# Scaling the second half's residual rows in products four and five of the down projections, and alternating rotary and gate items

## The chip, the core and the metric

The kernel runs on one core of a Trainium2 chip. The metric is device time in microseconds (us) of one execution, the median over runs. The engines by the names that the profile uses: PE multiplies matrices, DVE does elementwise work with one or two tensors as input, ACT elementwise functions of one tensor, POOL is a third elementwise engine, and SP issues most of the DMAs (POOL and ACT have DMA queues too). All work between PE's matmuls and the DMAs goes through SBUF, and PE's sums lie in PSUM.

## What is computed

Two layers over a sequence of 1024 rows of width 1024, in float32. Layer 0 mixes with a gated DeltaNet, layer 1 with retention; each is followed by a feed-forward block with a causal convolution of width 3 on its gate. The part of the reference that matters here:

```python
for i in range(DEPTH):
    mod = (e @ ada_w[i] + ada_b[i])[:, None, :]
    sh1, sc1, g1, sh2, sc2, g2 = jnp.split(mod, 6, axis=-1)
    y = mixers[i % N_MIXERS](x * (1.0 + sc1) + sh1)
    x = layer_norm(DN_ALPHA * x + (1.0 + g1) * y, ln_g[i, 0], ln_b[i, 0])
    y = conv_ffn(x * (1.0 + sc2) + sh2, ffn_up[i], ffn_conv_w[i], ffn_conv_b[i], ffn_down[i])
    x = layer_norm(DN_ALPHA * x + (1.0 + g2) * y, ln_g[i, 1], ln_b[i, 1])
```

`conv_ffn` is an up projection to 2 x 2816 columns, the convolution, `silu(gate) * up`, and a down projection from 2816 to 1024. Retention projects to queries, keys, values and a gate, turns queries and keys by rotary tables (`t1 * cos - t2 * sin`, `t1 * sin + t2 * cos`), and multiplies its output by `silu(gate)`.

## The kernel before, in words

A float32 matrix product is made of three matmuls. Each operand is split into a high and a low part: ACT copies it (L89) into a shorter float format, and DVE subtracts that copy from it (L90). Both read and write SBUF. The three products of high and low parts are summed in PSUM.

The large projections use the scheme of Strassen and Winograd: seven products of half-size blocks in place of eight, with sums of blocks as operands. `strassen` walks over a list of items, one for each pair of column blocks; `wino` makes the seven products of an item and hands the results in quadrants to the item's `sink`, which does what follows the projection. Of one item the weights are loaded and summed on DVE (L1213), split (L89, L90) and multiplied (84 matmuls, L110 to L112 and L1163), and the quadrants are put together on DVE (L1154).

**The feed-forward block.** The last sink of an up pair (`gated`, L1570ff) makes four blocks of `silu(gate) * up`, stores those three that the down projection needs as they are, and then makes four sums of them, on POOL for all pairs but the first (L1585), each stored too. The down projection is `proj_gen` (L1276ff): seven products, here numbered one to seven (`p` is 0 to 6 in the code), each of 11 steps (`nj`), each step of 12 matmuls (L285 to L287 or L1437). For a step `ops` loads a block `ar` of the stored activations (L1270), and takes a block of weights (loaded by L1303, summed on DVE at L1311 to L1317); both are split, `ar` into `ab` and the weights into `bb`. The steps' operands are prepared ahead of PE, as far as the number of buffers allows.

For the layer norm that follows, `xload` (L280) loads the residual rows: those of the first half are called up in product three, those of the second in product six. The residual is itself the output of a layer norm whose gain and bias are still to be applied. For rows of the first half `finish` applies them. For rows of the second half `gain_half(n)` (L1339 to L1346) does it in the background in eight pieces of 128 x 512: SP loads a piece (L1343), POOL multiplies by the row of gains and adds the row of biases (L1345 twice), and POOL's own DMA queue stores it (L1346), from where `xload(1, t)` reads it. The pieces are called up inside the loop over steps, in products one and two at every second step, and stand in `lane` buffers. The gain and bias rows occupy four `auh` buffers until the last piece is done. `gain_half` runs in both down projections, about 1198 to 1418 us and 2729 to 2948 us of the span. The second is the end of the program.

**The order of the work.** Engines execute in order; so does SP, so that a DMA that waits for a buffer holds up those behind it. The code is traced in the order written, with generators that interleave streams, and a scheduler then places the instructions by the data and buffers that they wait for. A tile is a numbered buffer of a named group (`lane`, `xT`, `auh`, `qkv`, ...); a new tile of a group waits until the oldest is free. The group `xT` (four tiles of 128 x 512) serves the opening of the kernel.

**Retention's projections of queries, keys and gate.** Layer 1 begins with a `strassen` list of 16 items, about 1450 to 1776 us: gates 0 and 2, then eight rotary items (`rope_item`, L1637ff: for each of two halves DVE does six operations with the rotary tables, L1651 to L1656, and ACT's queue stores the result, L1658), then gates 4 to 14 (`gate_item`, L1663ff: ACT applies Silu, L1667, and stores, L1668). The rotary tables `trig` (L1632) lie in `auh` buffers. `bg_step` calls up, between items, pieces of another background job: `unit` and `gain` (L387 to L395) scale the residual of the next layer norm on POOL as `gain_half` does, and need `auh` buffers for their two rows. The value products of retention (`ret_v`, L651) follow the list.

The lines that the steps of the prediction touch are L1343, L1345, L1346 (pieces), L1585 (sums), L89 and L90 (splits), L280 (residual rows), L1651 to L1656 (rotary tail), L387 and L393 to L395 (background scaling). In the program after the change all lines behind L1669 are three higher.

Of the kernel before, what the change touches and what calls it, by code (L numbers as in the profile page):

```python
# [15 lines left out]
P = 128  # L16
# [3 lines left out]
HALF = 512  # L20
NCH = S // P
GH = 8
RH = 4
# [10 lines left out]
def trunk_kernel(ctx: ExitStack, tc, A):  # L34
# [11 lines left out]
    def tl(tag, shape, dt=F32, name=None):  # L46
        return sb.tile(shape, dt, tag=tag, name=name or tag, bufs=BUFS[tag])
# [13 lines left out]
    def mm_tile():  # L61
        return ps.tile([P, HALF], F32, tag="mm", name="mm", bufs=2)

    def sc_tile():
        return ps.tile([P, HALF], F32, tag="sc", name="sc", bufs=2)

    def acc4():
        return [acc_tile(), acc_tile(), acc_tile(), acc_tile()]
# [13 lines left out]
    def hs(half):  # L82
        return slice(half * HALF, (half + 1) * HALF)
# [4 lines left out]
    def split(dst_h, dst_l, src, eng=dve):  # L88
        act.activation(dst_h, src, AF.Copy)  # L89
        eng.tensor_tensor(dst_l, src, dst_h, ALU.subtract)  # L90
# [3 lines left out]
    def after(key):  # L94
        return tc.issue_after(anchor[key].ins) if key in anchor else nullcontext()
# [12 lines left out]
    def mm3(acc, w, k, hl, first, last, mm=pe.matmul):  # L108
        wh, wl = w
        mm(acc, wl[:, k], hl[0], start=first, stop=False)  # L110
        mm(acc, wh[:, k], hl[1], start=False, stop=False)  # L111
        mm(acc, wh[:, k], hl[0], start=False, stop=last)  # L112
# [262 lines left out]
    xg = [dr.tile([S, D], F32, tag=f"xg{i}", name=f"xg{i}") for i in range(3)]  # L375
# [30 lines left out]

    def build_T(B, xts, scale, shift, tags):
        tags = dict(zip(("T1", "T2", "T3", "T4", "22"), tags))
        tags["12"] = tags["T1"]
        for nm in tags:  # L410
            B[nm] = [None] * 4

        def put(nm, k, src, eng=dve):
            t = two(tags[nm], F32R, nm)
            split(t[0], t[1], src, eng)
            B[nm][k] = t

# [18 lines left out]
        def whole(b, k):  # L436
            pt = mm_tile()
            for i, x in enumerate(B[b][k]):
                pe.matmul(pt, one, x, start=(i == 0), stop=(i == 1))
# [99 lines left out]
    xT = {}  # L539
# [166 lines left out]
    def take(tag, n):  # L706
        while free[tag] < n:
            yield lambda: free[tag] >= n
        free[tag] -= n

    def give(tag, n):
        free[tag] += n
# [444 lines left out]
    def strassen(hT0, xts, scale, shift, items, tags=("hTb", "hTb", "qkv", "qkv", "aux"), direct=False):  # L1157
        B = {"11": hT0[:4], "21": hT0[4:]}
        nblk = [0]
# [7 lines left out]
        def side(n, s):  # L1167
            out = []
            for u in items[n][:2]:
# [4 lines left out]
                for i, b in enumerate((("11", "21"), ("12", "22"))[s]):  # L1174
                    for k in range(4):
                        mm3(X, w, k + 4 * i, B[b][k], i == 0 and k == 0, i == 1 and k == 3)
                out.append(X)
# [96 lines left out]
    def proj_gen(nj, ablk, wsrc, slots, xsrc, G, final, ln_next, tag, ltags, dst, key, mm=pe.matmul, gate=None, gain=None):  # L1274
# [60 lines left out]
        xts = [[], []]  # L1335
# [2 lines left out]

        def gain_half(n):  # L1339
            hf, rs = n // 4, slice(HALF + n % 4 * P, HALF + (n % 4 + 1) * P)  # L1340
            x = tl("lane", [P, HALF], name="xg")
            with after("w"):
                sp.dma_start(x, gain[1][rs, hs(hf)])  # L1343
            for r, op in zip(grows, (ALU.mult, ALU.add)):
                pool.tensor_tensor(x, x, r[hf], op)  # L1345
            pool.dma_start(xsrc[rs, hs(hf)], x)  # L1346
# [10 lines left out]
        def finish(half, t, nh, c):  # L1357
            dve.tensor_tensor(c, c, G[nh], ALU.mult)
            xv = xts[half][t][:, hs(nh)]
            dve.scalar_tensor_tensor(xv, xv, ALPHA, c, ALU.mult, ALU.add)  # L1360
            dve.bn_stats(stats[half][t][:, nh], xv)
# [85 lines left out]
        for p, (an, bn, fin, side, fresh) in enumerate(prods):  # L1447
            if gate and p < 2 or banks[side] is None:
                banks[side] = acc4() if gate and p < 2 or side == 0 else [sc_tile(), sc_tile(), mm_tile(), mm_tile()]
                if gate and p == 1:  # L1450
                    banks[0] = banks[1]
                    banks[1] = None
            accs = banks[0] if gate and p == 1 else banks[side]
            tail = []
            depth = ltags[3] if p == 6 else 2
            for j in range(nj):
                if gate and p < 2:
                    yield gate(j)
                    yield from take("qkv", 2)
                    give("qkv", 2)  # L1460
                a, w = ops(an, bn, j, not gate and p < (7 if final else 5))
                with after("a"):
                    for st in steps[p * nj + j + ahead:p * nj + j + ahead + 1]:
                        load_b(*st)
                if gain and p < 2 and j % 2 == 0 and p * 4 + j // 2 < 8 and j < 8:
                    gain_half(p * 4 + j // 2)
                if gain and p == 2 and j % 2 == 0 and j < 8:
                    xload(0, j // 2)
                if p == 2 and j < 4 and gate:
                    xload(0, j)  # L1470
                    finish(0, j, 0, c11[j])
                if j >= nj - depth:
                    tail.append((j, a, w))
                else:
                    for t in range(4):
                        mma(accs[t], t, a, w, fresh and j == 0, False, mm if p < 2 else pe.matmul if fresh else mm_on)
                        yield 0.0
                for _ in range(-(-20 // (nj - 1)) if p == 6 else 4 if p == 5 else 2):
                    if later:
                        later.pop(0)()  # L1480
                if p == 5 and j > 1 and not later:
                    for _ in range(-(-16 // (nj - 2))):
                        if hooks:
                            hooks.pop(0)()
                bg_step()
            while later:
                later.pop(0)()
            if p == 5:
                while hooks:
                    hooks.pop(0)()  # L1490
            if p == 6:
                pin[0] = None
            for t in range(4):
                for j, a, w in tail:
                    mma(accs[t], t, a, w, fresh and j == 0, j == nj - 1, mm if p < 2 else pm_on if p == 6 else pe.matmul if fresh else mm_on)
                fin(t, accs[t])
                yield 0.0
            if p == 1:
                yield "P2"
            if p == 4:  # L1500
                hooks = [] if final else ln_hooks(0, xts[0], tag, ln_next, outs, dst, key, bal["h"])
                hooks += [lambda t=t: xload(1, t) for t in range(4)]
# [113 lines left out]
    h0, xts = layer_tail(0, raws, A["gdn_wout"], xin, xs[0], xs[1], next0, False)  # L1616
# [22 lines left out]
    def rope_item(h, j):  # L1639
        def start():  # L1640
            c = {}

            def sink(q, a, b):
                c[q] = c_of(q, a, b)
                hf = q % 2
                if hf not in c or hf + 2 not in c:
                    return
                x1, x2 = c[hf], c[hf + 2]
                cos, sin = trig(h, j)
                m = tl("lane", [P, 2, HALF], name="rm")  # L1650
                dve.tensor_mul(m[:, 0], x2, sin[hf])  # L1651
                dve.tensor_mul(m[:, 1], x1, sin[hf])
                dve.tensor_mul(x1, x1, cos[hf])
                dve.tensor_mul(x2, x2, cos[hf])
                dve.tensor_sub(x1, x1, m[:, 0])
                dve.tensor_add(x2, x2, m[:, 1])  # L1656
                for d, x in enumerate((x1, x2)):
                    act.dma_start(qd[j, h, d][:, hs(hf)], x)  # L1658
            return sink
        u = 8 * j + 2 * h  # L1660
        return A["ret_wqk"][u], A["ret_wqk"][u + 1], start, None

    def gate_item(u):
        def start():
            def sink(q, a, b):
                c = c_of(q, a, b) if b is not None else tl("cv", [P, 516], name="sg")[:, 0:HALF]
                act.activation(c, a if b is None else c, AF.Silu)  # L1667
                act.dma_start(gd[u + q // 2][:, hs(q % 2)], c)  # L1668
            return sink  # L1669
        return A["ret_wg"][u], A["ret_wg"][u + 1], start, None  # L1670

    sc_r, sh_r = next0()
    B = strassen(h0, xts, sc_r, sh_r, [gate_item(0), gate_item(2)]
                 + [rope_item(h, j) for h in range(RH) for j in range(2)] + [gate_item(u) for u in range(4, 16, 2)], ("hTa", "aux", "qkv", "qkv", "hTa"), True)
    hT = [h0, []]
    xlo = []
    for t in range(4):
        x = tl("cv", [P, 516], name="xlo")[:, 0:HALF]
# [270 lines left out]
```

## Time and profile before

| what | value |
|---|---|
| median of three runs | 2973.52 us (2968.97 to 2977.79) |
| span of the profiled execution | 2967.8 us |
| time of the profiled execution itself | not recorded beside its span |
| mean granted PE clock | 0.985 |
| ACT busy | 1316.5 us (44%) |
| moved by DMA | 451.01 MB, mean 152 GB/s |

The span runs from the first to the last instruction of one execution, so it is shorter than a timed run, which also holds what lies around it. The profile's page gives each engine's busy time, the span in 40 slices, the DMA queues, the chain of waits that ended last, and groups of equal instructions. The trace can be asked further: windows (busy time of each engine in a stretch, with the granted clock of PE as a share of full speed and the share of time in which the 16 DMA engines were busy), timelines (start, duration, engine, line, operation, output<-inputs, shape, and in brackets the idle time before it with what ended it), and groups by tile (count; least, median and largest duration in ns; first and last start).

### The profile page before, as it was taken

What the parts mean: (1) busy time and instruction counts of PE and PEld (TensorE: products, weight loads), DVE (VectorE), ACT (ScalarE), POOL (GpSimd) and SP (SyncE); (2) the same over time, 40 slices, a digit from 0 to 9 for tenths busy, and PEclk for the clock granted to TensorE, in tenths of its full rate; (3) what the DMA queues carried; (4) which work ended last, traced back from release to release, by engine and by line L of the source; (5) the groups of instructions that cost most, each with busy time, mean ns of one, the idle gap of its engine ahead of it and who ended that gap; (6) DMA issues with size and microseconds to landing.
All of it is one profiled execution on the core that took longest, in us unless ns stands there. A gap on an engine that the chain in (4) does not pass through costs nothing. (4 is left out here: it accounts for less than half of the span.)

```text
span 2967.8 us, 38939 instructions
## 1 busy us (share of the span) xinstructions
PE 2820.5 (95%) x13638; PEld 2304.5 (78%) x13638; DVE 2242.4 (76%) x4005; ACT 1316.5 (44%) x2413; POOL 474.8 (16%) x469
## 2 busy tenths in 40 slices
PE   8999898999999999999999999999999999999997
PEld 7887777887788888787877887777777788887786
DVE  5787787656688888879678645666689887777979
ACT  4744564444544444446433442222344544444443
POOL 0312221100001111610000202322202011112301
PEclk9999999999999999999999999999999999999998
DMA  7231222254245445865333544665664243335753
GB/s 275 79 113 65 86 79 79 83 167 160 91 158 163 158 151 174 305 198 179 120 128 117 181 160 152 203 189 175 205 212 157 91 135 107 107 107 176 274 183 137
DMA packets 244404, 451.01 MB, mean 152 GB/s; under 512 B 23088, under 2 KB 76592, under 8 KB 244208
## 3 DMA queue, kind: packets, MB, share of 16 engines
q1 hardware_dynamic: 213088, 401.07, 41.0%
q10 hardware_dynamic: 29760, 43.00, 4.0%
q0 software_dynamic: 1360, 4.46, 0.4%
q8 instruction: 107, 1.75, 0.3%
q14 instruction: 89, 0.73, 0.1%
HBM read 339.91 MB, written 108.53 MB: 151 GB/s over the span
## 5 line engine op out<-in xcount | busy, mean ns | idle before, releaser
L651 PE MATMUL acc<-hT,wh 128*128 128x512 f32 x960 | 299.3, 393 | 0.0
L1437 PE MATMUL acc<-bb,ab 128*128 128x512 f32 x984 | 231.4, 393 | 6.6 <-DVE bb L90 5.4
L1585 POOL TENSOR_TENSOR o<-o 128x512 f32<-128x512 f32 x80 | 110.7, 1394 | 716.4 <-DVE o L1578 490.8
L1437 PEld LDWEIGHTS acc<-bb,ab 128*128 128x128 f32 x984 | 182.6, 188 | 50.2 <-DVE bb L90 10.2
L1163 PE MATMUL acc<-T,wb 128*128 128x512 f32 x840 | 203.1, 391 | 6.7 <-DVE wb L90 6.7
L651 PEld LDWEIGHTS acc<-hT,wh 128*128 128x128 f32 x960 | 181.9, 190 | 34.1
L651 PE MATMUL acc<-hT,wl 128*128 128x512 f32 x480 | 201.1, 419 | 0.0
L89 ACT ACTIVATE ab<-ar 128x512 fp32r<-128x512 f32 x210 | 129.6, 625 | 152.7 <-PE mm L287 36.9
L90 DVE TENSOR_TENSOR ab<-ar,ab 128x512 fp32r<-128x512 f32 x210 | 161.9, 777 | 41.1 <-ACT ab L89 41.1
L1163 PEld LDWEIGHTS acc<-T,wb 128*128 128x128 f32 x840 | 157.0, 188 | 43.2 <-DVE wb L90 9.8
L90 DVE TENSOR_TENSOR wl<-wr,wh 128x1024 fp32r<-128x1024 f32 x95 | 119.7, 1260 | 69.6 <-ACT wh L89 68.6
L90 DVE TENSOR_TENSOR wb<-mm,wb 128x512 fp32r<-128x512 f32 x216 | 145.5, 682 | 31.2 <-ACT wb L89 30.6
L90 DVE TENSOR_TENSOR wb<-wr,wb 128x512 fp32r<-128x512 f32 x162 | 111.1, 691 | 69.8 <-ACT wb L89 69.1
L89 ACT ACTIVATE wh<-wr 128x1024 fp32r<-128x1024 f32 x95 | 100.7, 1061 | 132.3 <-PE acc L651 53.1
L1224 ACT ACTIVATE pc<-acc 128x512 f32<-128x512 f32 x143 | 84.9, 593 | 160.7 <-PE acc L1163 97.4
L1564 DVE SCALAR_TENSOR_TENSOR o<-g,vc,o 128x512 f32<-128x512 f32 (+2 forms) x176 | 145.4, 843 | 4.7 <-ACT o L1559 4.1
L89 ACT ACTIVATE wb<-mm 128x512 fp32r<-128x512 f32 x216 | 124.0, 595 | 51.9 <-DVE mm L1213 50.3
L89 ACT ACTIVATE wb<-wr 128x512 fp32r<-128x512 f32 x162 | 99.4, 628 | 104.0 <-DMA wr<-in_ffn_up 38.8
L651 PE MATMUL acc<-wh,hT 128*128 128x512 f32 x384 | 135.6, 415 | 1.6 <-DVE vv L90 1.6
L110 PE MATMUL acc<-T,wb 128*128 128x512 f32 x292 | 116.0, 397 | 9.4 <-DVE wb L90 9.4
L472 DVE SCALAR_TENSOR_TENSOR qkv<-raw,vc,qkv 128x512 f32<-128x512 f32 x144 | 111.6, 779 | 11.5 <-ACT qkv L470 10.7
L223 DVE SCALAR_TENSOR_TENSOR ada<-mvw,e,ada 128x512 f32<-128x512 f32 x140 | 106.9, 764 | 17.4 <-DMA mvw<-in_ada_w 17.1
(641 smaller groups left out, 7466.8 us busy)
## 6 DMA issues: line engine op xcount, KB each, us to landing
wr<-in_ffn_up SPq DMA_DIRECT2D x92, 512.0 KB, 4.4
mvw<-in_ada_w SPq DMA_DIRECT2D x80, 512.0 KB, 4.3
ad<-o SPq DMA_DIRECT2D x154, 256.0 KB, 3.1
ar<-ad SPq DMA_DIRECT2D x154, 256.0 KB, 3.9
Br<-in_ffn_down SPq DMA_DIRECT2D x88, 256.0 KB, 3.8
wr<-in_ret_wv SPq DMA_DIRECT2D x32, 512.0 KB, 3.9
ar<-od SPq DMA_DIRECT2D x56, 256.0 KB, 5.3
xs<-xt ACTq DMA_DIRECT2D x24, 512.0 KB, 3.7
```

The costliest lines, as they stand in the source:

```text
L89: act.activation(dst_h, src, AF.Copy)
L90: eng.tensor_tensor(dst_l, src, dst_h, ALU.subtract)
L110: mm(acc, wl[:, k], hl[0], start=first, stop=False)
L223: dve.scalar_tensor_tensor(a, wr[:, kk], e[:, k:k + 1], a, ALU.mult, ALU.add)
L472: dve.scalar_tensor_tensor(oh, raw[:, 3 - j:515 - j], w[:, 3 - j:4 - j], oh, ALU.mult, ALU.add)
L651: pq(pe.matmul(out, lhsT, rhs, start=start, stop=stop), cost)
L1163: return pe.matmul(*a, skip_group_check=True, **kw)
L1224: act.activation(t, X, AF.Copy)
L1437: return pe.matmul(*args, skip_group_check=True, **kw)
L1564: dve.scalar_tensor_tensor(tv, gv[:, c0 - j:c1 - j], w[:, 2 - j:3 - j], tv, ALU.mult, ALU.add)
L1585: (dve if fp == 0 else pool).tensor_tensor(o[d], o[x], o[y], op)
```

## The change

There are two parts. In `proj_gen`, `gain_half` is called in products four and five (`p` 3 and 4) in place of one and two, and its tile is taken from the group `xT` in place of `lane`. In the retention's list of items, the eight rotary items and six gate items no longer stand in two blocks: after gates 0 and 2 come one rotary item, three times (rotary, gate), one rotary item, and three times (rotary, gate), so that a gate ends the list.

```diff
         def gain_half(n):
             hf, rs = n // 4, slice(HALF + n % 4 * P, HALF + (n % 4 + 1) * P)
-            x = tl("lane", [P, HALF], name="xg")
+            x = tl("xT", [P, HALF], name="xg")
             with after("w"):
                 sp.dma_start(x, gain[1][rs, hs(hf)])
...
-                if gain and p < 2 and j % 2 == 0 and p * 4 + j // 2 < 8 and j < 8:
-                    gain_half(p * 4 + j // 2)
+                if gain and p in (3, 4) and j % 2 == 0 and j < 8:
+                    gain_half((p - 3) * 4 + j // 2)
                 if gain and p == 2 and j % 2 == 0 and j < 8:
                     xload(0, j // 2)
...
-    B = strassen(h0, xts, sc_r, sh_r, [gate_item(0), gate_item(2)]
-                 + [rope_item(h, j) for h in range(RH) for j in range(2)] + [gate_item(u) for u in range(4, 16, 2)], ("hTa", "aux", "qkv", "qkv", "hTa"), True)
+    ropes = [rope_item(h, j) for h in range(RH) for j in range(2)]
+    gates_ = [gate_item(u) for u in range(4, 16, 2)]
+    mixed = [ropes.pop(0)] + [r for k in range(3) for r in (ropes.pop(0), gates_.pop(0))] + [ropes.pop(0)]
+    mixed += [r for k in range(3) for r in (ropes.pop(0), gates_.pop(0))]
+    B = strassen(h0, xts, sc_r, sh_r, [gate_item(0), gate_item(2)] + mixed, ("hTa", "aux", "qkv", "qkv", "hTa"), True)
```

The diff leaves `gain_half`'s loads, operations and stores, the sinks and the number of instructions as they are.

## The prediction

> **What bounds the kernel now.** I read the page first (busy shares, chain), then the windows around the two openings of the down projections, then the timeline of PE, DVE and POOL there, and last the rotary stage.
>
> ```profile
> span 2967.8 us, 38939 instructions
> ...
> PE 2820.5 (95%) x13638; PEld 2304.5 (78%) x13638; DVE 2242.4 (76%) x4005; ACT 1316.5 (44%) x2413; POOL 474.8 (16%) x469
> ...
> PE 24%; DVE 6%; DMA 4%; issue 1%; POOL 1%; ACT 1%; SPq 0%; ACTq 0%; DVEq 0%; POOLq 0%
> ```
>
> PE is busy for 95% and leads the chain of waits, so the time is the number of matmuls, plus the 2967.8 - 2820.5 = 147 us in which PE stands, plus what a halved clock costs. The change touches no matmul. What it can win are stalls, and it can only lose by making new ones. No time of the profiled execution is given beside its span. The span is 5.7 us under the median of the three runs (2973.52). I take that offset as constant, and add a difference worked out on the span to the median.
>
> The first stage that the diff touches is the opening of each down projection. The windows give, per stretch, its length, then busy us of PE, PEld, DVE, ACT and POOL, the granted clock, the DMA share and GB/s; first the opening in layer 0, then that in layer 1.
>
> ```profile
> 1200.00:1205.00 5.00, 3.79 (x17) 2.83 (x16) 3.86 (x5) 4.52 (x15) 4.58 (x4) 1.00 1.05 393
> 1205.00:1210.00 5.00, 2.18 (x10) 1.48 (x9) 5.00 (x7) 3.48 (x7) 4.90 (x6) 1.00 1.05 392
> 1210.00:1215.00 5.00, 2.49 (x10) 1.73 (x9) 5.00 (x2) 1.67 (x3) 4.98 (x6) 0.94 1.05 405
> 1215.00:1220.00 5.00, 4.54 (x15) 3.33 (x14) 5.00 (x5) 1.06 (x3) 3.50 (x4) 0.72 1.05 385
> ```
> ```profile
> 2730.00:2740.00 10.00, 7.71 (x32) 5.69 (x32) 8.68 (x10) 6.90 (x13) 8.75 (x8) 1.00 1.03 374
> 2740.00:2750.00 10.00, 6.85 (x28) 4.72 (x26) 10.00 (x6) 3.81 (x7) 9.98 (x8) 1.00 1.05 401
> 2750.00:2760.00 10.00, 9.79 (x36) 7.95 (x37) 9.22 (x11) 0.93 (x2) 6.54 (x6) 0.83 1.03 383
> ```
>
> PE stands for 20 - 13.00 = 7.00 us in the first and 30 - 24.35 = 5.65 us in the second. The clock costs (1 - 0.94) x 5 + (1 - 0.72) x 5 = 1.70 us and (1 - 0.83) x 10 = 1.70 us more. Together the two openings lose **16.05 us**. The timeline names what PE waits for (in brackets the idle before, and its releaser), and what DVE and POOL do then:
>
> ```profile
> 1208.76 0.50 PE L285 MATMUL acc<-bb,ab 128*128 128x512 f32 x1 [2.82 <-DVE ab L90]
> ...
> 1214.31 0.78 PE L285 MATMUL acc<-bb,ab 128*128 128x512 f32 x1 [2.51 <-DVE ab L90]
> ```
> ```profile
> 1207.47 6.78 DVE L90 TENSOR_TENSOR ab<-ar,ab 128x512 fp32r<-128x512 f32 x2
> 1214.18 3.84 DVE L260 TENSOR_TENSOR fh<-fh,v 128x8 f32<-128x8 f32 x1
> ```
> ```profile
> 1206.89 1.26 POOL L1585 TENSOR_TENSOR o<-o 128x512 f32<-128x512 f32 x1
> ...
> 1208.70 1.31 POOL L1345 TENSOR_TENSOR xg<-xg,rowb 128x512 f32<-128x512 f32 x1
> 1209.96 1.30 POOL L1585 TENSOR_TENSOR o<-o 128x512 f32<-128x512 f32 x1
> 1211.21 2.49 POOL L1345 TENSOR_TENSOR xg<-xg,rowb 128x512 f32<-128x512 f32 x2
> ...
> 1215.48 2.50 POOL L1585 TENSOR_TENSOR o<-o 128x512 f32<-128x512 f32 x2
> ```
> ```profile
> 1252.13 22.40 POOL L1345 TENSOR_TENSOR xg<-xg,rowb 128x512 f32<-128x512 f32 x2 [6.62 <-DMA xg<-xs]
> ```
> ```profile
> 1254.14 1.27 DVE L90 TENSOR_TENSOR ab<-ar,ab 128x512 fp32r<-128x512 f32 x2
> ```
>
> PE waits for DVE's split of `ar`. Two such splits take 1.27 us at 1254 and 6.78 us at 1207; an addition of 8 columns takes 3.84 us while POOL runs back to back. The reverse also shows: at 1252 POOL's two operations last 22.40 us while DVE runs without a gap. So DVE and POOL shut each other out, and whichever is in possession keeps it while its queue is full. In the opening POOL is in possession, with the scaled residual pieces (L1345) and the last sums of the up projection (L1585).
>
> **The change part by part.** *Pieces leave the opening.* The row of tile `xg` counts the operations:
>
> ```profile
> L1345 POOL TENSOR_TENSOR xg<-xg,rowb x32: 1257/1625/20702, 1199.6 to 2782.6; 128x512 f32<-128x512 f32 x32
> L1343 SPq DMA_DIRECT2D xg<-xs x16: 319/339/430, 1194.4 to 2773.5; - x16
> ```
>
> For each down projection that is 16 POOL operations, 8 loads and (L1346, on POOL's queue) 8 stores of 256 KB. In the four windows of the first opening POOL is busy 17.96 us; the four sums of L1585 shown above are 4 x 1.3 = 5.2 us of them, and they alone remain. DVE itself has 5 + 7 + 2 + 5 = 19 instructions in the 20 us, which at the 0.64 us of the 1254 row are 12.2 us; so it has 7.8 us to spare against 5.2. But PE follows the splits with hardly a step in hand there, so a block of two sums (2.50 us at 1215.48) can still show. Shared out by POOL's time, 5.2/17.96 of 16.05 = 4.65 us would stay (the second opening taken as the first); if the spare time covers them, nothing. I take 2.0 us per opening, 4.0 in all, near the upper end because the stretches that stall PE most hold both kinds: **gain 16.05 - 4.0 = 12.0 us**, bounds 11.4 and 16.05. The loads and stores gone (16 x 256 KB = 4.2 MB at some 390 GB/s, 10.8 us of a saturated DMA at share 1.05) give a further reason why `ar` comes earlier, and no further term. Should the DMA and not POOL be what held the splits up, the gain shrinks; that is a rival below.
>
> On the clock: both dips follow a gap under 3 us (2.51 and 2.64 us in the timeline of before). The Trainium skill ("TensorE: Matmul & The Clock Gate", section "HAM oscillation — how this bites in real kernels") says that PE gaps above about 3.4 us are what brings the clock down; by that no dip should be here, and the trace disagrees. By the trace a rest of 2.5 us could still bring a dip in each opening: the sum would be 12.0 - 3.4 = 8.6 us.
>
> *Pieces arrive in products four and five.* In the changed program's order the eight loads stand after the 34th to the 51st load of `ar`. Before, that 51st was issued at 1306:
>
> ```profile
> 1305.99 0.33 SPq L1270 DMA_DIRECT2D ar<-ad  x1
> ```
> ```profile
> 1315.55 0.69 DVE L90 TENSOR_TENSOR ab<-ar,ab 128x512 fp32r<-128x512 f32 x1 [1.43 <-ACT ab L89]
> ...
> 1331.01 0.39 PE L285 MATMUL sc<-bb,ab 128*128 128x512 f32 x1
> ```
> ```profile
> 1300.00:1310.00 10.00, 10.00 (x46) 8.29 (x45) 5.17 (x8) 4.58 (x10) 0.00 (x0) 1.00 0.76 234
> 1310.00:1320.00 10.00, 10.00 (x46) 8.29 (x45) 6.23 (x10) 4.06 (x8) 0.00 (x0) 1.00 0.63 188
> 1320.00:1330.00 10.00, 10.00 (x46) 8.29 (x45) 8.13 (x14) 4.50 (x8) 0.00 (x0) 1.00 0.52 158
> 1330.00:1340.00 10.00, 10.00 (x46) 8.29 (x45) 10.00 (x18) 3.35 (x7) 0.00 (x0) 1.00 0.34 107
> ...
> 1360.00:1370.00 10.00, 8.35 (x36) 6.39 (x35) 10.00 (x20) 3.46 (x6) 1.00 (x1) 1.00 0.47 132
> ```
>
> The split for the 46th step ends at 1316.2 and PE uses it at 1331.0: a lead of 15 us, held by buffers. DVE is 5.2 and 6.2 of 10 busy, so it has 4.8 + 3.8 us free in 20. A piece blocks DVE for 2 x 1.3 = 2.6 us, every two splits (5.4 us of PE), four pieces 10.4 us; the lead and the free time take it: **cost 0**. Without that cover it is 2.6 us a piece. The DMA share is 0.5 to 0.8 there, so 0.25 MB per 5.4 us (47 GB/s) has room. POOL has nothing else to do (0.00). Behind the added wait on SP (a buffer of the opening, free since the opening; later pieces wait for the store of the piece four before) stand `ar` loads, and the same lead of 15 us covers a delay of theirs. The row loads of the gains hold their buffers longer, and the rotary tables come later in SP's queue, but their use begins with the rotary items (the 1529 row below), some 200 us on: cost 0. The residual's first half (L280) is loaded a few `ar` loads earlier: 0.
>
> *Rotary and gate items alternate.* The timeline shows a stall after each of the eight rotary items, the first with a regular length and the last:
>
> ```profile
> 1529.07 3.06 PE L1163 MATMUL acc<-T,wb 128*128 128x512 f32 x12 [1.06 <-DVE wb L90]
> ...
> 1651.51 1.66 PE L1163 MATMUL acc<-T,wb 128*128 128x512 f32 x6 [1.06 <-DVE wb L90]
> ```
> ```profile
> 1527.73 0.68 DVE L1656 TENSOR_TENSOR pc<-pc,rm 128x512 f32<-128x512 f32 x1
> 1528.33 1.28 DVE L90 TENSOR_TENSOR wb<-mm,wb 128x512 fp32r<-128x512 f32 x2
> ```
> ```profile
> 1500.00:1530.00 30.00, 28.34 (x124) 22.84 (x123) 26.27 (x43) 9.63 (x18) 0.00 (x0) 1.00 0.37 123
> ...
> 1710.00:1740.00 30.00, 30.00 (x134) 24.85 (x133) 13.55 (x22) 12.60 (x23) 0.00 (x0) 1.00 0.31 109
> ```
>
> DVE is not full here (26.3 of 30): the split that PE needs stands in DVE's queue behind the rotary tail of the item before (L1651 to L1656). In the changed order the same run of tail operations stands ahead of the same split after every rotary item, whether a gate or a rotary item follows. So I expect eight stalls again, in other places: **0**. At most all eight go. An item with its stall takes (1651.51 - 1529.07) / 6 = 20.41 us; at the pace of the window at 1710 (134 matmuls in 30 us) its 84 matmuls take 18.8. So all eight are worth 8 x 1.06 = 8.5 to 8 x 1.6 = 12.9 us; between them I take 10.6. Less than 0 has a bound of the same kind, if DVE met POOL there, which it does not now.
>
> *The scaling of the layer's first residual* (L387, L393 to L395) waits for buffers of the rotary tables; as the last rotary item is now the fifteenth of 16 and was the tenth, they begin some five items of 19 us later than 1641, at about 1738.
>
> ```profile
> L393 POOL TENSOR_TENSOR xg<-xg,gb x16: 1262/1295/1319, 1641.4 to 1900.8; 128x512 f32<-128x512 f32 x16
> ...
> 1663.29 0.50 PE L110 MATMUL acc<-hT,wb 128*128 128x512 f32 x1 [0.60 <-DVE wb L90]
> ...
> 1785.49 0.50 PE L651 MATMUL acc<-wh,hT 128*128 128x512 f32 x1 [0.97 <-DVE vv L90]
> ```
>
> It takes the 0.60 us at 1663.29 with it; their blocks of 2.6 us (two operations) then lie near the start of the retention's value products, where PE already waits 0.97 us for DVE. Between -0.6 and +5 (two blocks in full); DVE is only 13.55 of 30 busy from 1710 on, so I take **+0.5**.
>
> Sum: -12.0 + 0 + 0 + 0.5 = -11.5, and 2973.5 - 11.5 = **2962.0 us**.
>
> **The rivals.** *B: the rotary stalls go too.* DVE's 13.55 of 30 in gate items speaks for it, the unchanged order of the tail against it: 2962.0 - 10.6 = 2951.4. *C: the sums of L1585 and the full DMA keep most of the opening's loss* (two dips and two thirds of the idle, 3.4 + 8.4 of 16.05): share 1.05 for 20 us speaks for it, the 1.27 against 6.78 us of a split against it; gain 4, 2969.5. *E: the moved first residual costs its two blocks*, 5.2 where I took 0.5: 2966.7. *D, slower: the block returns in products five and six.* The exclusion goes along with the pieces; the Trainium skill ("SBUF — State Buffer", section "🔬 SBUF: two separate sides") says the same: an operation of VectorE with two inputs in SBUF and one of GpSimd that reads SBUF lock each other out, and the later one is blocked in full. The 6.78 us above agree. The cover ends at 1330, where DVE is 10.00 of 10, and PE already waits at 1360 to 1370 (8.35). If SP is held up so that the last four loads are issued after 1330 (2860 in layer 1), four blocks of 2.6 us come through in each down projection, 20.8 us, with a dip of 1.70 in each, 24.2: 2973.5 + 24.2 - 11.5 = 2986. Against it stands the 1306 above, 24 us early. *The change not doing what it says* is excluded for the order: the pieces, loads and items do stand elsewhere.
>
> **How the numbers follow.** Forecast 0.52, B 0.11, C 0.19, E 0.08, D 0.10. A measurement of this kernel tells about 0.3% (8.9 us) from no change, so faster is under 2964.6, which lies only 2.6 us above the forecast. Of the forecast 0.36 falls under it, with B 0.11, C 0.02 and E 0.03: faster 0.52. D gives slower 0.09; same 0.39. Range: B at its end and the bounds (16.05 and -0.6 give 2956.9) reach down to 2950, C and E with the three runs' own spread up to 2977; D is left out (0.10), with some 0.08 of tails.
>
> **What would show it.** Right: in 1198 to 1222 and 2730 to 2756 the splits of `ar` take about 0.7 us each, the clock stays at 1.00, and PE idles under 3 us; no L1345 before the fourth product's loads; the windows to 1330 and 2860 keep PE at 10.00; eight stalls of 1.06 us behind rotary items, some 40 us apart in the alternation. Wrong: DVE splits of 2 us or more in products four to six beside L1345 (D); the old gaps with POOL idle (C); no stalls behind rotary items (B); a new gap at 1735 to 1810 (E).

## The result, and the profile after

Measured in the same rounds, the changed kernel takes 2966.41 us (median of 6 runs, 2960.09 to 2969.90) and the kernel before 2975.67 us (6 runs, 2968.97 to 2980.50): a ratio of 0.9973 with a 95% interval of 0.9960 to 0.9986. Timed once more later it came to 2962.26 us against 2974.94 us, ratio 0.9960 (0.9947 to 0.9974). So by the ratios it is faster by 8 to 12 us, and the forecast of 2962.0 us, a ratio of 0.9961 to the median of 2973.52 us that stood before it, lies there. But the way to that number was another than forecast.

The page of the changed kernel (first execution):

```profile
span 2966.1 us, 38887 instructions
...
PE 2823.3 (95%) x13638; PEld 2306.3 (78%) x13638; DVE 2245.0 (76%) x4005; ACT 1317.3 (44%) x2413; POOL 470.9 (16%) x469
...
PE 74%; DVE 11%; DMA 6%; ACT 4%; issue 3%; POOL 2%; SPq 0%; ACTq 0%; POOLq 0%; DVEq 0%
```

The sums have not moved, and the span of this pair of profiles is only 1.7 us shorter. A page does not show why. Both programs issue the same 13,638 matmuls, so the start of the n-th matmul can be compared in both traces. The table does this for all kernels of this study. A number is what a kernel loses (or, negative, gains) against the profiled execution of before between two matmuls. The starts of before are at the top.

| from matmul to matmul | 6000-6600 | 6600-7200 | 7500-8400 | 8400-9300 | 9300-10800 | 12600-13200 | all |
|---|---|---|---|---|---|---|---|
| time in before (us) | 1145.7-1290.7 | 1290.7-1428.4 | 1495.7-1711.0 | 1711.0-1917.3 | 1917.3-2286.7 | 2703.8-2848.5 | to 2948.7 |
| stage | first opening | products 4 to 7 | rotary, gate | first values | retention | second opening | |
| before, once more | -0.2 | 0.0 | -0.5 | -3.8 | 5.4 | -1.1 | 1.4 |
| after | -9.5 | 10.1 | -4.1 | 3.7 | 5.4 | -8.7 | -0.9 |
| after, once more | -9.7 | 7.1 | -4.1 | 5.0 | 3.2 | -8.7 | -8.7 |
| pieces only | -9.7 | 10.2 | -0.2 | -3.0 | 1.8 | -8.7 | -8.7 |
| list only | 2.1 | -0.2 | -4.0 | 6.7 | 4.4 | 0.8 | 7.9 |
| after, tables by POOL's queue | -9.8 | 3.5 | -3.2 | 6.4 | 5.6 | -8.7 | -6.5 |
| pieces, tables by POOL's queue | -9.0 | 4.1 | 1.0 | 1.0 | 7.4 | -8.7 | -4.3 |
| pieces, tables late | -9.7 | 1.6 | -0.5 | -1.7 | 5.0 | -8.4 | -17.9 |
| pieces, tables late, list with three pairs | -9.8 | 1.8 | -2.3 | 2.1 | 4.7 | -8.5 | -14.5 |
| after, tables late | -9.8 | 1.4 | -4.1 | 7.4 | 2.4 | -8.3 | -13.6 |
| the same, scaling by POOL's queue | -9.6 | 0.9 | -4.1 | 12.3 | 6.0 | -8.6 | -5.9 |
| pieces, POOL work in the openings | 0.5 | 4.1 | -0.2 | -2.4 | 5.3 | -5.5 | 1.4 |
| pieces, DMA in the openings | -5.2 | 10.3 | -0.4 | -0.6 | 6.7 | -7.6 | 0.7 |

Every other kernel, before itself included, loses 2 to 7 us against this execution from 9300 to 10800. The profiled execution of before was a lucky one there, and a sum over one pair of traces misleads by that much. Most stages repeat better: the two executions of before agree to about 1 us at the openings. Two do not: from 8400 to 9300 these two differ by 3.8 us, and from 6600 to 7200 the two executions of after differ by 3.0 us. "All" also holds what lies outside the columns, above all the time up to matmul 6000, where the kernels stand between -4.4 and +1.3 us against before. At the openings, after waits no more. Its windows, with the columns as before:

```profile
1200.00:1210.00 10.00, 10.00 (x46) 8.27 (x45) 10.00 (x17) 8.96 (x23) 3.00 (x2) 1.00 1.03 383
1210.00:1220.00 10.00, 10.00 (x46) 8.29 (x45) 10.00 (x17) 5.63 (x10) 8.89 (x1) 1.00 1.04 390
1310.00:1320.00 10.00, 8.62 (x39) 6.80 (x37) 3.76 (x6) 4.33 (x8) 2.36 (x3) 1.00 0.70 229
1320.00:1330.00 10.00, 4.98 (x12) 3.95 (x13) 8.96 (x16) 0.17 (x1) 0.00 (x0) 0.54 0.41 131
```
```profile
2730.00:2740.00 10.00, 10.00 (x46) 8.29 (x45) 6.14 (x10) 5.27 (x10) 0.00 (x0) 1.00 0.83 276
2740.00:2750.00 10.00, 10.00 (x46) 8.29 (x45) 10.00 (x13) 6.74 (x13) 5.89 (x4) 1.00 1.05 397
2750.00:2760.00 10.00, 10.00 (x45) 8.28 (x45) 10.00 (x16) 3.74 (x7) 0.70 (x1) 1.00 1.05 393
```

In both openings PE is full and the clock whole, although the DMA share is about as high as before (1.03 to 1.05, and 0.83 in the first window of the second opening). New is a hole at 1310 to 1330 in layer 0, where before PE was full. It lies between the fourth and the fifth product. The timeline of the changed kernel shows it on PE, then on DVE, SP and POOL:

```profile
1325.02 0.77 PE L285 MATMUL sc<-bb,ab 128*128 128x512 f32 x1 [6.39 <-DVE u L1410]
```
```profile
1305.34 3.48 DVE L90 TENSOR_TENSOR ab<-ar,ab 128x512 fp32r<-128x512 f32 x2
1314.08 0.69 DVE L1317 TENSOR_TENSOR Br<-Bw,Br 128x512 f32<-128x512 f32 x1 [5.26 <-DMA Br<-in_ffn_down]
...
1318.14 0.69 DVE L1317 TENSOR_TENSOR Br<-Bw,Br 128x512 f32<-128x512 f32 x1 [2.16 <-DMA Br<-in_ffn_down]
```
```profile
1304.96 0.32 SPq L1270 DMA_DIRECT2D ar<-ad  x1
1310.51 0.33 SPq L1632 DMA_DIRECT2D trig<-in_trig  x1
1310.93 0.38 SPq L1303 DMA_DIRECT2D Br<-in_ffn_down  x1
1311.88 0.33 SPq L1632 DMA_DIRECT2D trig<-in_trig  x1
1312.30 0.38 SPq L1270 DMA_DIRECT2D ar<-ad  x1
```
```profile
1309.18 2.68 POOL L1345 TENSOR_TENSOR xg<-xg,rowb 128x512 f32<-128x512 f32 x2
```

The bracket on PE names DVE's L1410, which empties the sums `sc` of the fourth product; in DVE's order it stands behind the splits and subtractions that come late. DVE does not wait for POOL there, but for weights (`Br`) that have not landed. Their load stands in SP's queue behind a load of a rotary table (`trig`, L1632). SP issues nothing from 1305.3 to 1310.5. The table's buffer is one of the four `auh` buffers with the gain and bias rows, and POOL gives up the first when the multiplication of the last piece ends (the first half of the 2.68 us from 1309.18) and the second when the addition ends at 1311.86. The two table loads leave at just these times. PE loses 6.39 us, and the clock is halved until 1331.

This wait of 5.2 us is the second of its kind. The first two table loads wait in the same way for the gain and bias rows of the first half, on SP and POOL:

```profile
1270.79 1.10 SPq L1270 DMA_DIRECT2D ar<-ad  x1
1284.33 0.33 SPq L1632 DMA_DIRECT2D trig<-in_trigq  x1
```
```profile
1261.58 13.84 POOL L1345 TENSOR_TENSOR xg<-xg,rowb 128x512 f32<-128x512 f32 x2 [33.62 <-DMA xg<-xs]
...
1281.77 2.53 POOL L1345 TENSOR_TENSOR xg<-xg,rowb 128x512 f32<-128x512 f32 x2
```

SP issues nothing from 1271.9 to 1284.3, 12.4 us, until the multiplication of the fourth piece has ended at 1284.30. The pieces are later than they need be because DVE in its turn shuts POOL out: the first piece takes 13.84 us, during which DVE runs almost without a gap, where two operations alone take about 2.5. This longer wait shows no gap on PE, but it makes the loads of activations, weights and the next pieces late, and so it is likely that it used up the lead that would have covered the second wait.

### The profile page after: what moved, and what is told of

Same layout as the page of the kernel before. It is cut to its first block, busy times and chain, and to the rows that moved or that the text cites. A ratio compares the mean times of both kernels' runs of the same rounds, so it can differ in the third digit from the quotient of the medians.

```text
span 2966.1 us, 38887 instructions
## 1 busy us (share of the span) xinstructions
PE 2823.3 (95%) x13638; PEld 2306.3 (78%) x13638; DVE 2245.0 (76%) x4005; ACT 1317.3 (44%) x2413; POOL 470.9 (16%) x469
## 4 chain that ended last, share of the span: by engine, by line
PE 74%; DVE 11%; DMA 6%; ACT 4%; issue 3%; POOL 2%; SPq 0%; ACTq 0%; POOLq 0%; DVEq 0%
PE acc L651 15%; PE acc L1163 10%; PE acc L110 6%; PE acc L111 6%; PE acc L112 5%; PE sc L1163 5%; PE sc L651 4%; PE acc L1437 3%; PE mm L651 2%; PE sc L111 2%; PE sc L112 2%; PE sc L110 2%; DMA Br<-in_ffn_down 1%; DVE bb L90 1%; DVE ab L90 1%
## 5 line engine op out<-in xcount | busy, mean ns | idle before, releaser
L1585 POOL TENSOR_TENSOR o<-o 128x512 f32<-128x512 f32 x80 | 126.1, 1586 | 793.9 <-DVE o L1578 458.5
L223 DVE SCALAR_TENSOR_TENSOR ada<-mvw,e,ada 128x512 f32<-128x512 f32 x140 | 106.3, 759 | 17.9 <-DMA mvw<-in_ada_w 17.5
```

The source lines that it names most:

```text
L223: dve.scalar_tensor_tensor(a, wr[:, kk], e[:, k:k + 1], a, ALU.mult, ALU.add)
L1585: (dve if fp == 0 else pool).tensor_tensor(o[d], o[x], o[y], op)
```

## The experiments

My theory after the result had three parts: (1) POOL's operations in the openings cost 18 us, because DVE is shut out; (2) the pieces' new place lets SP stand in front of the table loads; (3) the new list gains in the rotary stage and loses about as much at the value products. The rivals: that the alternation carries the gain, that the full DMA made the opening's loss, and that exclusion in product four makes the hole.

**Each part alone.** The first two kernels hold the first and the second part of the diff shown above, one each.

> Only the pieces of gain_half are moved; the list of items is as before. Theory: both openings lose nothing (about -10 us at the first, -9 us at the second, by matmul starts), and SP's wait for the buffers of the rotary tables, which the later pieces hold, costs about +9.5 us in product four of the first down projection only; so about -9 us in all, ratio to before 0.997, with the PE gap of about 6 us near 1318 there. Rival (the alternation of the list is what made the kernel faster): within 3 us of before, ratio 0.999 to 1.001.

Measured: 2956.53 us (6 runs, 2951.69 to 2964.78), before 2971.96, ratio 0.9948 (0.9930 to 0.9967). That is more than the -9 expected. By matmul starts the profiled execution does show what was expected: -9.7, -8.7 and a hole of 10.2, in all -8.7 against the lucky execution of before. That execution took 2960.57 us, 4 us more than the median.

> Only the list of retention's items alternates; the pieces stay in products one and two. Theory: six of the eight stalls behind rotary items are 0.77 us where they were 1.22 us, and one of 0.77 us at 1663 goes, about -4 us; the background scaling moves next to the first value products and costs about +5; sum within 2 us of before, ratio 0.9993 to 1.0007, both openings with their gaps. Rival (the alternation carries the gain): ratio 0.997.

Measured: 2974.98 us (12 runs), ratio 1.0009 (0.9997 to 1.0020). The list gains nothing, and it may cost a little; its rival is out. Its two halves show in the table: -4.0 and +6.7, the second in the stage where two executions of before differ by 3.8.

**The tables on another queue.** In both kernels the loads of the tables go by POOL's queue; the first has the whole change, the second the pieces alone.

```diff
-                    sp.dma_start(t[hf], (A["trig"][i] if j else A["trigq"][h, i])[:, hs(hf)])
+                    pool.dma_start(t[hf], (A["trig"][i] if j else A["trigq"][h, i])[:, hs(hf)])
```

> The whole change, and the rotary tables are loaded by POOL's DMA queue in place of SP's. Theory (SP stands in front of a table load until the pieces give up the gain rows' buffers, and the loads of activations and weights behind it come late): the gap of 6.4 us near 1318 and the slow clock behind it go, about -9 us against the whole change, ratio to before 0.994, about 2957 us. Rival (DVE and POOL shut each other out in product four, so that the splits are late): the gap stays, ratio 0.997.

Measured: 2960.74 us, ratio 0.9957 (0.9940 to 0.9974). The hole shrinks from 7 to 10 us to 3.5, less than expected.

> The pieces moved, the list as before, the rotary tables loaded by POOL's DMA queue. Theory: both openings' gain of about 18 us is kept whole, ratio 0.994, about 2956 us; this is the fastest of the four if the alternation is worth nothing. Rival (the gap in product four does not come from SP's queue): ratio 0.997, as the pieces alone.

Measured: 2957.64 us, ratio 0.9951 (0.9934 to 0.9968), no better than the pieces alone. The stage from 6600 on still loses 4.1 us, now in a gap of 3.95 us at 1357.74 in product six. The loads of tables still come between the pieces and their stores, and the scheduler has put the rest in another order. So these two runs support (2) without settling it.

**The tables behind everything.** With the pieces as in the change and the old list, each table load is placed behind the last load of activations of the first down projection, on SP as before.

```diff
-                    sp.dma_start(t[hf], (A["trig"][i] if j else A["trigq"][h, i])[:, hs(hf)])
+                    with after("w"):
+                        sp.dma_start(t[hf], (A["trig"][i] if j else A["trigq"][h, i])[:, hs(hf)])
```

> The pieces moved, list as before, and the loads of the rotary tables placed on SP behind the last load of activations of the first down projection. Theory (SP stood in front of a table load): the gap of 6 us near 1318 and its slow clock go, about -9 us against the pieces alone by matmul starts and 2948 us or a ratio of 0.992. Rival (DVE and POOL contend in product four, the tables are incidental): the gap stays, ratio 0.995.

Measured: 2952.24 us (5 runs, 2951.01 to 2956.72), ratio 0.9938 (0.9924 to 0.9951); 2948 was expected. This is the fastest kernel of the study. The hole is gone, though the pieces have the same place in the program (the last four run 5 to 9 us earlier against PE, and further apart, since SP no longer waits); its windows:

```profile
1300.00:1310.00 10.00, 10.00 (x45) 8.28 (x45) 6.36 (x11) 4.59 (x8) 3.83 (x3) 1.00 0.79 265
1310.00:1320.00 10.00, 10.00 (x45) 8.26 (x44) 9.90 (x17) 2.23 (x5) 0.00 (x0) 1.00 0.39 112
1320.00:1330.00 10.00, 10.00 (x46) 8.28 (x45) 10.00 (x18) 4.51 (x8) 0.00 (x0) 1.00 0.55 188
```

So the wait of SP made the hole, and the exclusion in product four costs PE nothing here. By matmul starts this is worth 8.6 us against the pieces alone (1.6 against 10.2), by the medians only 4, with intervals that overlap; whether the hole is as large in every execution of the pieces alone stays open. It is in both profiles of after (10.1 and 7.1) and in that of the pieces alone. The next two kernels also keep the tables on SP at their old place and bear on it: where SP waited 8.4 and 5.0 us for the tables' buffers (DMA in the openings) the hole is 10.3 us, and where it waited 2.2 and 2.5 us (POOL work in the openings) the stage loses only 4.1 us.

**What fills the openings.** Both kernels have the pieces in their new place and the old list, and give back one half of the old load at the old place: the first 16 operations of POOL on rows in SBUF, whose result nothing uses, the second the loads and stores, to a scratch tensor.

```diff
+        def dummy(n):
+            x = tl("lane", [P, HALF], name="dm2")
+            pool.tensor_tensor(x, grows[0][n // 4], grows[1][n // 4], ALU.mult)
+            pool.tensor_tensor(x, x, grows[1][n // 4], ALU.add)
...
+                if gain and p < 2 and j % 2 == 0 and j < 8:
+                    dummy(p * 4 + j // 2)
```

> The pieces moved as in the change (list as before), and in the openings 16 operations of POOL of the pieces' shape on rows that lie in SBUF, with no DMA; their result is used by nothing. Theory (POOL and DVE shut each other out): the splits last 2 to 7 us again, PE loses 5 us or more at each opening against the pieces alone, though less data moves. Rival (it was the 4.2 MB of DMA): the openings stay without a gap.

Measured: one run, 2971.35 us. The first opening loses 10.2 us against the pieces alone (0.5 against -9.7), the whole of what the change had won there; the second 3.2, less than the 5 us expected. POOL and DVE in the first opening:

```profile
1200.17 1.25 POOL L1350 TENSOR_TENSOR dm<-rowb 128x512 f32<-128x512 f32 x1
1201.39 1.73 POOL L1351 TENSOR_TENSOR dm<-dm,rowb 128x512 f32<-128x512 f32 x1
1203.08 3.42 POOL L1350 TENSOR_TENSOR dm<-rowb 128x512 f32<-128x512 f32 x2
```
```profile
1200.32 3.35 DVE L90 TENSOR_TENSOR ab<-ar,ab 128x512 fp32r<-128x512 f32 x2
1203.60 3.45 DVE L90 TENSOR_TENSOR bb<-Bw,bb 128x512 fp32r<-128x512 f32 x2
```

Two splits last 3.4 us with no byte of the pieces moving. Since this kernel's operations need no data, they begin earlier than those of before (the first at 1184.75 against 1199.58, in the second opening at 2717.20 against 2730.13) and stand closer, so the load on POOL is not at quite the old place.

```diff
...
+            with after("w"):
+                sp.dma_start(x, gain[1][rs, hs(hf)])
+            pool.dma_start(scr[rs, hs(hf)], x)
...
```

> The pieces moved as in the change (list as before), and in the openings the eight loads and eight stores of 256 KB of the kernel before, to a scratch tensor that nothing reads, with no operation of POOL between. Theory (exclusion): PE loses under 2 us at each opening, the splits keep their 0.7 us. Rival (the full DMA kept the splits waiting): PE loses 5 us or more, with DVE and POOL idle.

Measured: one run, 2969.09 us. The first opening loses 4.5 us against the pieces alone (-5.2 against -9.7), the second 1.1. Neither theory had this. The loss is one gap and a dip of the clock behind it, and the gap's rows on PE, DVE and POOL are these:

```profile
1203.94 0.50 PE L285 MATMUL acc<-bb,ab 128*128 128x512 f32 x1 [2.46 <-DVE ab L90]
```
```profile
1202.53 3.06 DVE L90 TENSOR_TENSOR ab<-ar,ab 128x512 fp32r<-128x512 f32 x2
```
```profile
1202.08 2.96 POOL L1595 TENSOR_TENSOR o<-o 128x512 f32<-128x512 f32 x2 [1.53 <-issue]
```

It is again a split beside POOL, here beside two of the sums (L1585 before, L1595 in this kernel). In the changed kernel two such sums take 3.08 us at 1204.40, and a pair of splits 2.38 us, and PE does not notice. My reading is that the added transfers make the loads of activations late and so take away the step in hand that covers such a block: the fifth of these loads leaves SP 5.8 us after the first (1196.22, 1190.39), with the pieces alone 3.8 us (1196.09, 1192.34). In the second opening the two halves come to 3.2 + 1.1 = 4.3 us of the 8.7; what brings the rest, both together or the earlier start of POOL's work, was not tried.

**The list.** Two kernels with the late table loads and different lists. The first has three (rotary, gate) pairs, five rotary items, three gates; the second the list of the change.

```diff
-    B = strassen(h0, xts, sc_r, sh_r, [gate_item(0), gate_item(2)]
-                 + [rope_item(h, j) for h in range(RH) for j in range(2)] + [gate_item(u) for u in range(4, 16, 2)], ("hTa", "aux", "qkv", "qkv", "hTa"), True)
+    mixed = [r for k in range(3) for r in (ropes[k], gates_[k])] + ropes[3:] + gates_[3:]
+    B = strassen(h0, xts, sc_r, sh_r, [gate_item(0), gate_item(2)] + mixed, ("hTa", "aux", "qkv", "qkv", "hTa"), True)
```

> As the run with the late table loads, and a list with three (rotary, gate) pairs, then five rotary items, then three gates. Theory (a rotary item behind a gate costs 0.77 us of stall where one behind a rotary item costs 1.22; what the alternation loses is the background scaling beside the first value products): three stalls fewer of the long kind, -1.4 us, and the first value products lose nothing, since the scaling comes some 57 us before them: within 2 us of the late table loads alone, a little faster by matmul starts. Rival (any rotary item moved back costs): slower by 3 us.

Measured: 2954.67 us, ratio 0.9940 (0.9927 to 0.9952), as the late tables alone within the interval. By stages -2.3 (-0.5 with the old list) and 2.1 (-1.7).

> The whole change (pieces and alternating list) with the table loads behind the last load of activations. Theory (the list is worth about -4 us in the rotary stage and about +7 us at the first value products): some 3 us slower than the pieces with late tables alone, ratio to before about 0.995, with PE gaps between 1740 and 1790 that the kernel with the old list does not have. Rival (the list only did harm together with the wait for the tables): as the pieces with late tables alone, ratio 0.9938.

Measured: 2961.18 us, ratio 0.9961 (0.9946 to 0.9975) against 0.9938 without the list. The stages are -4.1 and +7.4, against -0.5 and -1.7 without the list, so the list costs 5.5 us by the stages and 7 us by the ratios. The later the last rotary item, the dearer the stage of the first value products: tenth item -1.7, thirteenth 2.1, fifteenth 7.4, one execution each. Part of this is spread: the stage also holds later waits of retention, in which two executions of before differ by 3.8 us. The waits at the first value products alone come to 2.9 us in the changed kernel:

```profile
1756.88 0.44 PE L266 MATMUL mm<-cst,xlo 128*128 128x128 f32 x2 [1.05 <-DMA xlo<-xs]
1758.39 0.50 PE L651 MATMUL acc<-wh,hT 128*128 128x512 f32 x1 [1.07 <-ACT wh L89]
1759.65 0.50 PE L651 MATMUL acc<-wl,hT 128*128 128x512 f32 x1 [0.76 <-DVE wl L90]
```

In the next kernel the background scaling's loads and stores go by POOL's queue.

```diff
-            sp.dma_start(x, src[rs, hs(c)])
+            pool.dma_start(x, src[rs, hs(c)])
...
-            sp.dma_start(dst[rs, hs(c)], x)
+            pool.dma_start(dst[rs, hs(c)], x)
```

> As the whole change with late table loads, and the loads and stores of the background scaling (L387 and L395) go by POOL's DMA queue in place of SP's. Theory (SP's queue: the rows for the value products, L1681 in the kernel before, stand behind stores that wait for POOL): the loss of about 7 us at the first value products goes for the greater part, ratio about 0.993. Rival (DVE and POOL shut each other out there): it stays, ratio 0.995.

Measured: 2962.45 us, ratio 0.9961 (0.9947 to 0.9976); the stage loses 12.3 us, not less (part of it again in later waits, of 3.54 us at 1828 and 3.66 us at 1867). The theory that SP stands behind the scaling's stores falls, since the waits at the first value products do not shrink either: 1.76, 2.25 and 0.77 us here, 0.47, 1.07 and 0.76 with the scaling on SP. PE there waits for the rows and then for the first weights of the value products:

```profile
1745.14 0.44 PE L266 MATMUL mm<-cst,xlo 128*128 128x128 f32 x2 [1.76 <-DMA xlo<-xs]
1747.83 0.49 PE L651 MATMUL acc<-wh,hT 128*128 128x512 f32 x1 [2.25 <-ACT wh L89]
```

SP's queue in this kernel, and then in the one with the old list and late tables:

```profile
1733.21 1.33 SPq L1823 DMA_DIRECT2D qk<-qd  x3
1740.34 0.32 SPq L1685 DMA_DIRECT2D xlo<-xs  x1
1740.75 1.88 SPq L102 DMA_DIRECT2D wr<-in_ret_wv  x2
```
```profile
1732.45 0.33 SPq L102 DMA_DIRECT2D wr<-in_ret_wv  x1
1735.47 1.33 SPq L1820 DMA_DIRECT2D qk<-qd  x3
```

With the old list the first weights (L102) leave at 1732, ahead of the loads of finished queries and keys (`qk`); with the alternation they come 8 us later, behind such loads, which read what the last rotary item has stored. That points to this order as the cause. It was argued from these rows and not tried by itself.

**The two kernels once more.**

> The kernel before, profiled once more, for the spread of one execution. If the profiled execution of before was a fast one between 1900 and 2300 us, this one loses 2 to 5 us against it there, as all the changed kernels did; the openings show the same gaps to within 1 us.

Measured: one run, 2970.10 us; it loses 5.4 us from 9300 to 10800, and -0.2 and -1.1 at the openings. Not expected was a gain of 3.8 us from 8400 to 9300.

> The kernel after the change, timed in the same rounds. From the parts (pieces 0.9948, list 1.0009) its ratio is 0.9957; from its first measurement 0.9973. The sum of parts theory takes 0.996 with both inside the intervals; if the parts disturb each other it stays at 0.997 or above. Its gap before product five is there again.

Measured: 2962.26 us, ratio 0.9960 (0.9947 to 0.9974), the sum of the parts (0.9957) to 0.0003; the first measurement, 0.9973, lies further off, with an interval that starts at 0.9960. Its hole costs 7.1 us.

## Why the prediction was right, and where it was wrong

The number was right by two errors that cancel.

- **Pieces leave the opening: mechanism right, size too small.** I took 12.0 us of 16.05. By matmul starts the openings lost 9.7 + 8.7 = 18.4 us, and all of it went. The windows had shown less, 16.05 us, since they count as busy the whole record of the last matmul before a gap (some 0.4 us, where the next one otherwise starts after 0.23) and the slow first one behind it. The 2.0 us per opening that I left for the sums of L1585 were nothing: PE is full beside them. Rival C (the full DMA) holds in part, since the transfers alone bring 4.5 and 1.1 us back; POOL's operations alone bring 10.2 and 3.2.
- **Clock.** No dip is left in the openings, as taken; the case of 8.6 us did not come.
- **Pieces arrive in products four and five: exclusion right, "cost 0" wrong.** The lead and DVE's free time cover the 2.6 us of each piece, as the late-table kernel shows with PE at 10.00. The step that failed is the sentence that the gain rows "hold their buffers longer, and the rotary tables come later in SP's queue", priced at 0 because the tables are first used some 200 us on. I priced the late use of the table and not the queue behind its load: SP issues in order, and the loads of activations and weights behind it waited 12.4 and then 5.2 us. That cost 7 to 10 us in layer 0. Nor did I see that DVE, by shutting POOL out, would make the first pieces late and so hold the rows still longer. In layer 1, which has no table loads, there is no hole.
- **Rival D** named the right place and sign, not the mechanism: products four to six lose in layer 0, but by SP's queue; the long splits of its sign are there (3.48 us for two at 1305), but in the late-table kernel such splits (1.66 and 1.78 us for one at 1296 and 1298) cost PE nothing.
- **Alternation: eight stalls, right; equal size, wrong.** A rotary item that follows a gate costs less than one that follows a rotary item. In the changed kernel's timeline, first behind a rotary item with another one before it, then behind one with a gate before it:

```profile
1529.35 3.01 PE L1163 MATMUL acc<-T,wb 128*128 128x512 f32 x12 [1.06 <-DVE wb L90]
...
1568.33 1.88 PE L1163 MATMUL sc<-T,wb 128*128 128x512 f32 x7 [0.61 <-DVE wb L90]
```

  Two stalls keep 1.06 us of idle and six have about 0.61, where before seven had 1.06. With the stall at 1663 gone, and one of the six now behind the end of that stage of the table, that is the -4.1 us that I had at 0. Rival B (all eight go) is out.
- **The first residual's scaling: +0.5 taken, too small.** From 8400 to 9300 kernels with the full alternation lose 3.7 to 7.4 us (the one with POOL's queue 12.3), those with the old list -3.8 to 1.0. Rival E had the place and the size (5.2). Its mechanism, two blocks of POOL against DVE, is not what the rows show: PE waits for rows and weights. The 3.7 to 7.4 us hold the spread of this stage too.

In sum: -18.4 where -12.0 stood, +7 to +10 where 0 stood, and -4 and +4 to +7 where 0 and +0.5 stood. That these add up to the forecast's 11.5 us or near it is luck.

## What to carry to other kernels

A buffer that is held longer is paid by the next instruction that wants it, and, on a queue that issues in order, by everything behind that instruction; price that queue and not the late use of the data. Work off the critical path is free where the bounding engine has steps in hand and dear where it has none, so move it to a stretch with a lead and then look for who waits for what it holds. Where two programs issue the same instructions on the bounding engine, compare the start of the n-th instruction in both traces, and profile the kernel before twice, ahead of trusting a sum over one pair.

## What the runs showed of the hardware

DVE and POOL do not only shut each other out for long stretches. With full queues on both sides they also take turns: in the kernel with POOL work in the openings two POOL operations took 3.42 us and two splits beside them 3.45 us, 1.7 us for a turn of one each, where alone they take about 1.25 and 0.64. That is less than the sum of 1.89, so a little of each does overlap. In the same place before, two splits took 6.78 us.

The clock of PE can fall while PE still waits, and stay down longer than one dip. In the changed kernel the window from 1320 to 1330 has a granted clock of 0.54, so 9.2 of its 10 us were at half: it fell at about 1320.8, some 2.2 us into the gap of 6.39 us, and the matmuls run slow until about 1331, 10.2 us in all. In the same kernel profiled once more, behind a gap of 5.91 us, it was half for 6.8 us. The dips in the openings before last 3.4 us each (1.70 us lost at half clock). The length of a gap alone does not decide: behind the 2.82 us that end at 1208.76 no dip follows, behind the 2.51 us that end at 1214.31 one does.
